# Half a line of 64 bytes ahead of the weight units and of one half of h

## The chip, the cores and the metric

The kernel runs on one core of one Trainium2 chip. The metric is the device time of one execution in microseconds (us), as the median of several runs. On this core TensorE (PE) does the matmuls, with its weight loads shown apart (PEld); VectorE (DVE), ScalarE (ACT) and GpSimd (POOL) do elementwise work; SyncE (SP) issues most of the DMAs.

## The reference

One layer of an encoder on 256 tokens of width 2048, in float32, with post-norm and a residual factor ALPHA = 2**0.25:

```
x <- LN1(ALPHA*x + 0.5 * (silu(x @ w_gate1) * (x @ w_up1)) @ w_down1)      # 2048 -> 5632 -> 2048
p  = x @ w_in                                                              # 2048 -> 6144
y  = [hyena(p[:, :3072]) ; differential attention, 8 heads (p[:, 3072:])]
x <- LN2(ALPHA*x + y @ w_out)
x <- LN3(ALPHA*x + 0.5 * (silu(x @ w_gate2) * (x @ w_up2)) @ w_down2)
```

The two feed-forward blocks (5632 = 44 blocks of 128 wide) hold most of the arithmetic.

## The kernel before

**Float32 products out of rounded halves.** Every operand of a large matmul is held as two tiles of the type float32r: a high half `hi` (ScalarE's cast, L176, L102) and a low half `lo` = value minus `hi` (L177 on VectorE, or L99 on VectorE or GpSimd). A product is three matmuls, high by high, high by low, low by high (`mm3`, L93 to L96).

**Units.** All weights stream through SBUF in units of 512 KB (4,096 bytes in each of the 128 partitions), in an order written out by hand in the list `units`. `fetch` (L158 to L160) puts the DMA of a unit on SP's queue, into one of four `raw` buffers; `prepare` (L172 to L177) splits it into one of four `whi` and one of four `wlo` buffers. `nextunit` asks for transfers five units ahead and for splits two units ahead. The splits of four of the last eight units go into room of `xx` instead.

**Two ways round.** In the gate and up projections of both feed-forward blocks (groups `ps`) and in the Hyena part of w_in (groups `ph`), `ws_block` makes the weight unit the stationary operand and the turned x the moving one. `xx` holds, for each of 16 blocks of 128 features, the high half (256 tokens) and the low half (256 tokens) side by side, so that two matmuls do the three products: 512 columns with the unit's high half (L395) and 256 columns with its low half (L396). In the down projections (`pd`), the attention part of w_in (`pa`) and w_out (`pwo`) it is the other way round: the stationary operand is a block of tokens of `hh` and `hl` (the two halves of the feed-forward's h), of `xx`, or of the mixer's outputs, and the unit moves, 512 or 256 columns at a time, through the three matmuls L94 (high, high), L95 (high, unit's low) and L96 (low, unit's high).

**What else runs.** Beside the stream of matmuls, the generators in `side` are stepped once for each unit: filters and Hyena's transforms, softmax, layer norms, gates. Temporaries of 2,048 bytes share eight buffers with the tag `t512`.

**Places.** SBUF is given out pool by pool, in a row: `const`, then `wp` (the units), then `sm` (first the `t512` buffers, then `space`, then the smaller temporaries), then the pool of the stage (`fp` of a feed-forward block with `hh` and `hl`, or the pools of the mixer). A tile called `space` is written and read by nobody; it only moves what follows:

```
    line(const, 384 - 32 - 256)
    ...
    line(sm, 384)
```

In the program of before, all tiles that this change touches begin at a multiple of 128 bytes in the partition: `xx` at 35,328, the `raw`, `whi` and `wlo` buffers from 68,096 on in steps of 4,096, `t512` from 117,248 on, `hh` at 138,752 and `hl` at 183,808. The slices of them that a matmul reads lie whole multiples of 512 bytes behind these starts.

Of the kernel before, what the change touches and what calls it, by code (L numbers as in the profile page):

```python
# [11 lines left out]
F32 = mybir.dt.float32  # L12
# [5 lines left out]
P = 128  # L18
# [56 lines left out]
def kernel(ctx: ExitStack, tc: tile.TileContext, a: dict, out: bass.AP):  # L75
    nc = tc.nc

    const = ctx.enter_context(tc.tile_pool(name="const", bufs=1))
    wp = ctx.enter_context(tc.tile_pool(name="wp", bufs=4))
    sm = ctx.enter_context(tc.tile_pool(name="sm", bufs=2))  # L80
# [3 lines left out]
    def bank(name):  # L84
        return psp.tile([P, 512], F32, tag="ps", name=name)

    def line(pool, n):

        pool.tile([P, n // 4], F32, name="space", tag="space", bufs=1)

    mm = nc.tensor.matmul

# [8 lines left out]
    def split(o_hi, o_lo, x, eng=None):  # L101
        nc.scalar.copy(out=o_hi, in_=x)  # L102
        sub(eng or nc.vector, o_lo, x, o_hi)
# [85 lines left out]
    def beside(gen):  # L189
        side.append([0, gen])  # L190
# [11 lines left out]
    def once(f, *args):  # L202
        def g():
            f(*args)
            return
            yield
        beside(g())

    def nextunit():
        i = st["use"]  # L210
        st["use"] += 1
        fetch(i + 1 + AHEAD)
        prepare(i + 1 + READY)
        tick()
        return parts.pop(i)

    def finish_side():
        while side:
            tick()


    mhalf = const.tile([P, 2], F32, name="mhalf")
    stats = const.tile([P, 2, 5, 6], F32, name="stats")
    line(const, 384 - 32 - 256)
    ident = const.tile([P, P], F32, name="ident")
    ones = const.tile([P, P], F32, name="ones")
# [2 lines left out]

    res = const.tile([P, 2, D], F32, name="res")  # L230
    xx = const.tile([P, KD, 2, L], F32R, name="xx")
    xv = a["x"][0].rearrange("(p j) d -> p j d", j=2)
    xt0 = []
    for kp in range(KD // 2):
# [6 lines left out]
        if kp % 2 == 0:  # L241
            fetch(kp // 2 + 1)

    line(sm, 384)
    make_identity(nc, ident)
    nc.gpsimd.memset(ones, 1.0)
    nc.gpsimd.memset(mhalf, -0.5)
# [112 lines left out]
    def last_rows(tag, pd, scale, between=None):  # L360

        ln = []
        add_rows(pd[0], 0, 3, scale)
        ln.append(ln_stats(tag, 0))
        for half in range(2):
            add_rows(pd[1][half], 1, 3, scale, half)
            if between is not None and half == 0:
                between()
        ln.append(ln_stats(tag, 1))
        if tag == "2":  # L370
            warm(WARM)
        return ln
# [14 lines left out]
    def ws_block(ps, h, lo, kq, between=None):  # L387

        for k in range(4):
            kk = kq * 4 + k  # L390
            if k == 2 and between is not None:
                between()
            for t in range(2):
                ts_ = slice(t * P, (t + 1) * P)
                mm(out=ps[t], lhsT=h[:, k, ts_], rhs=xx[:, kk].rearrange("p a l -> p (a l)"), start=kk == 0, stop=False)  # L395
                mm(out=ps[t][:, :L], lhsT=lo[:, k, ts_], rhs=xx[:, kk, 0, :], start=False, stop=kk == KD - 1)  # L396

    def ws_sum(o, ps):
        nc.scalar.copy(out=o, in_=ps[:, L:])
        nc.vector.tensor_tensor(out=o, in0=ps[:, :L], in1=o, op=ALU.add)  # L400
# [18 lines left out]
    def last_banks(name):  # L419
        return [bank(f"{name}_0"), [bank(f"{name}_1{h}") for h in range(2)]]  # L420

    def as_chunk(pd, lhs, n_k, lead=1):

        n = n_k // 2
        for ku in range(n - lead):
            as_block(pd, lhs, [(ku * 2, nextunit())], n_k)
        use = [(ku * 2, nextunit()) for ku in range(n - lead, n)]
        as_block(pd, lhs, use, n_k, True)


    def ffn(tag, first, down_side=None, gate_side=None, filler=None, lead=2, between=None):
        with tc.tile_pool(name=f"ffn{tag}", bufs=1, reuse_waits="tile") as fp:
            hh = fp.tile([P, KF, L], F32R, name=f"hh{tag}")
            hl = fp.tile([P, KF, L], F32R, name=f"hl{tag}")

            def gate(f, pg, pu):
                sg = sm.tile([P, L], F32, tag="sg", name=f"sg{tag}_{f}")
                ws_sum(sg, pg)
                nc.scalar.activation(out=sg, in_=sg, func=AF.Silu)
                hf = sm.tile([P, L], F32, tag="hf", name=f"hf{tag}_{f}")  # L440
                ws_sum(hf, pu)
                nc.gpsimd.tensor_tensor(out=hf, in0=hf, in1=sg, op=ALU.mult)  # L442
                split(hh[:, f, :], hl[:, f, :], hf, nc.gpsimd)

            first(0)
            for fb in range(FF // 256):
                if fb == 12 and gate_side is not None:
                    beside(gate_side)
                ps = [[bank(f"ps{tag}_{fb}_{m}_{t}") for t in range(2)] for m in range(2)]
                for kq in range(4):  # L450
                    for m in range(2):
                        more = fb == 0 and kq < 3 and m == 0
                        ws_block(ps[m], *nextunit(), kq, (lambda: first(kq + 1)) if more else None)
                for t in range(2):
                    once(gate, fb * 2 + t, ps[0][t], ps[1][t])
            if down_side is not None:
                beside(down_side)

            def lhs(k, j):
                js = slice(j * P, (j + 1) * P)  # L460
                return hh[:, k, js], hl[:, k, js]

            for c in range(4):
                pd = [bank(f"pd{tag}_{c}_{j}") for j in range(2)] if c < 3 else last_banks(f"pd{tag}_{c}")
                as_chunk(pd, lhs, KF, lead if c == 3 else 1)
                if c < 3:
                    for j in range(2):
                        once(add_rows, pd[j], j, c, 0.5)
            finish_side()
            if filler is not None:  # L470
                filler()
            return last_rows(tag, pd, 0.5, between)
# [173 lines left out]
    def rows_of_x():  # L646
# [4 lines left out]
        yield from scale_residual("0", None, None)  # L651

    ln = ffn("1", first0, filter_gen(), filter_net(), fill)
    xn1 = dr.tile([P, 2, D], F32, name="xn1")

# [419 lines left out]
    def last_side():  # L1075
        yield from last_vectors()
        yield 1
        ln_rows()

    ln = ffn("3", first2, last_side(), lead=LEAD, between=early_g)  # L1080
    ov = out[0].rearrange("(p j) d -> p j d", j=2)

# [57 lines left out]
```

## Time and profile before

| | |
|---|---|
| median of 3 runs | 1944.33 us (1944.19 to 1946.62) |
| the profiled execution: its own time | 1943.8 us |
| its span, first to last instruction | 1942.0 us |
| granted TensorE clock | 0.998 |
| PE busy | 1922.5 us, 99% of the span, 10,582 matmul records |
| DVE, ACT, POOL busy | 63%, 48%, 16% |
| DMA | 376.50 MB, 194 GB/s on average |

The profile's rows name an instruction by its line (L395), engine, operation and tiles (out<-in). A group's row gives the count, the busy time in us, the mean of one instruction in ns, and the idle time of the engine ahead of them with what ended it. Matmuls are pipelined: the duration of one is longer than the distance from its start to the next one's start, and it is the distance that counts for the time.

### The profile page before, as it was taken

To read this page: it belongs to the slowest core of one execution; us is meant where nothing else is said; L and a number is where in the kernel's file an instruction comes from. 1 tells how busy PE (TensorE), PEld (TensorE's weight loads), DVE (VectorE), ACT (ScalarE), POOL (GpSimd) and SP (SyncE) were. 2 spreads that over 40 slices of the span, in tenths; PEclk is the share of its full clock that TensorE was granted. 3 is DMA by queue.
4 is the path that set the end of the run, shared out by engine and by line. 5 is a ranking of instruction groups with operands and counts; after the bars stand their busy time and mean duration, and the time that the engine had idled before them with its cause. 6 is when DMAs were issued, how large, how long until landed. Compare 5 with 4: busy or idle time off the path is not lost. (4 is left out here: it accounts for less than half of the span.)

```text
span 1942.0 us, 27741 instructions
## 1 busy us (share of the span) xinstructions
PE 1922.5 (99%) x10582; PEld 1659.8 (85%) x10582; DVE 1214.3 (63%) x1552; ACT 925.7 (48%) x1336; POOL 302.9 (16%) x335
## 2 busy tenths in 40 slices
PE   9999999999999999999999999999999999999998
PEld 8888888888888888888888888888888888888887
DVE  5555556555566656899978766755555555545545
ACT  5454444455444434554555544545444455433332
POOL 4212111112100001112222011311211112200000
PEclk9999999999999999999999999999999999999999
DMA  8665656565666665755575444856665655566653
GB/s 289 203 194 185 194 187 199 187 193 185 205 207 227 212 190 198 234 181 166 175 218 165 160 157 158 279 188 192 188 193 187 193 187 187 189 199 195 194 188 129
DMA packets 295278, 376.50 MB, mean 194 GB/s; under 512 B 13583, under 2 KB 223144, under 8 KB 295144
## 3 DMA queue, kind: packets, MB, share of 16 engines
q1 hardware_dynamic: 289720, 361.37, 58.5%
q0 software_dynamic: 4992, 12.82, 2.1%
q8 instruction: 83, 1.36, 0.3%
q10 hardware_dynamic: 432, 0.52, 0.1%
q14 instruction: 51, 0.42, 0.1%
HBM read 366.28 MB, written 8.39 MB: 193 GB/s over the span
## 5 line engine op out<-in xcount | busy, mean ns | idle before, releaser
L395 PE MATMUL ps<-xx,hi1g 128*128 128x512 f32 x1408 | 489.8, 394 | 0.8 <-ACT hi1g L176 0.8
L395 PE MATMUL ps<-xx,hi2g 128*128 128x512 f32 x1408 | 488.6, 394 | 1.1 <-DVE xx L99 1.1
L396 PE MATMUL ps<-xx,lo1g 128*128 128x256 f32 x1408 | 391.5, 279 | 1.1 <-DVE lo1g L177 1.1
L396 PE MATMUL ps<-xx,lo2g 128*128 128x256 f32 x1408 | 390.0, 277 | 0.0
L177 DVE TENSOR_TENSOR lo2g<-raw2g,hi2g 128x1024 fp32r<-128x1024 f32 x176 | 235.0, 1337 | 179.6 <-ACT hi2g L176 179.6
L177 DVE TENSOR_TENSOR lo1g<-raw1g,hi1g 128x1024 fp32r<-128x1024 f32 (+1 forms) x180 | 232.7, 1295 | 178.4 <-ACT hi1g L176 178.2
L395 PEld LDWEIGHTS ps<-xx,hi2g 128*128 128x128 f32 x1408 | 264.0, 188 | 62.5 <-ACT xt L305 1.3
L395 PEld LDWEIGHTS ps<-xx,hi1g 128*128 128x128 f32 x1408 | 263.8, 188 | 62.1 <-ACT hi1g L176 1.5
L176 ACT CAST hi2g<-raw2g 128x1024 fp32r<-128x1024 f32 x176 | 185.2, 1053 | 186.6 <-PE ps L395 174.9
L176 ACT CAST hi1g<-raw1g 128x1024 fp32r<-128x1024 f32 (+1 forms) x180 | 185.8, 1034 | 180.9 <-PE ps L395 170.4
L396 PEld LDWEIGHTS ps<-xx,lo1g 128*128 128x128 f32 x1408 | 265.2, 188 | 2.2 <-DVE lo1g L177 1.9
L396 PEld LDWEIGHTS ps<-xx,lo2g 128*128 128x128 f32 x1408 | 264.2, 188 | 0.1
L442 POOL TENSOR_TENSOR hf<-hf,sg 128x256 f32<-128x256 f32 x88 | 65.3, 761 | 741.9 <-DVE hf L400 741.8
L177 DVE TENSOR_TENSOR lo2d<-raw2d,hi2d 128x1024 fp32r<-128x1024 f32 x84 | 103.3, 1229 | 111.2 <-ACT hi2d L176 111.0
L176 ACT CAST hi1d<-raw1d 128x1024 fp32r<-128x1024 f32 x88 | 92.6, 1053 | 127.5 <-PE pd L96 117.0
L177 DVE TENSOR_TENSOR lo1d<-raw1d,hi1d 128x1024 fp32r<-128x1024 f32 x88 | 107.3, 1222 | 69.6 <-ACT hi1d L176 69.6
L176 ACT CAST hi2d<-raw2d 128x1024 fp32r<-128x1024 f32 x84 | 88.6, 1054 | 130.1 <-PE pd L96 123.2
L95 PE MATMUL pd<-lo1d,hh 128*128 128x512 f32 (+1 forms) x396 | 145.2, 367 | 0.0
L94 PE MATMUL pd<-hi1d,hh 128*128 128x512 f32 (+1 forms) x396 | 145.1, 366 | 0.0
L96 PE MATMUL pd<-hi1d,hl 128*128 128x512 f32 (+1 forms) x396 | 144.8, 366 | 0.0
L395 PE MATMUL ph<-xx,hihy 128*128 128x512 f32 x384 | 136.9, 400 | 2.1 <-DVE xx L99 1.1
L95 PE MATMUL pd<-lo2d,hh 128*128 128x512 f32 (+1 forms) x372 | 137.3, 369 | 0.0
(387 smaller groups left out, 3151.9 us busy)
## 6 DMA issues: line engine op xcount, KB each, us to landing
raw1d<-in_ffn_w_down_dram SPq DMA_DIRECT2D x88, 512.0 KB, 3.9
raw2g<-in_ffn_w_gate_dram SPq DMA_DIRECT2D x88, 512.0 KB, 3.5
raw2g<-in_ffn_w_up_dram SPq DMA_DIRECT2D x88, 512.0 KB, 3.4
raw2d<-in_ffn_w_down_dram SPq DMA_DIRECT2D x88, 512.0 KB, 4.1
raw1g<-in_ffn_w_gate_dram SPq DMA_DIRECT2D x87, 512.0 KB, 4.2
raw1g<-in_ffn_w_up_dram SPq DMA_DIRECT2D x87, 512.0 KB, 3.9
rawhy<-in_w_in_dram SPq DMA_DIRECT2D x48, 512.0 KB, 4.0
rawat<-in_w_in_dram SPq DMA_DIRECT2D x48, 512.0 KB, 4.2
```

The source lines that it names most:

```text
L94: mm(out=o, lhsT=lh, rhs=rh, start=start, stop=False)
L95: mm(out=o, lhsT=lh, rhs=rl, start=False, stop=False)
L96: mm(out=o, lhsT=ll, rhs=rh, start=False, stop=stop)
L176: i1 = nc.scalar.copy(out=hi[:, s_], in_=raw[:, s_])
L177: i2 = nc.vector.tensor_tensor(out=lo[:, s_], in0=raw[:, s_], in1=hi[:, s_].bitcast(F32), op=ALU.subtract)
L395: mm(out=ps[t], lhsT=h[:, k, ts_], rhs=xx[:, kk].rearrange("p a l -> p (a l)"), start=kk == 0, stop=False)
L396: mm(out=ps[t][:, :L], lhsT=lo[:, k, ts_], rhs=xx[:, kk, 0, :], start=False, stop=kk == KD - 1)
L442: nc.gpsimd.tensor_tensor(out=hf, in0=hf, in1=sg, op=ALU.mult)
```

## The change

Three tiles of padding are changed; no instruction is added, removed or moved. A tile of 64 bytes, tag `half`, comes behind `xx` in the pool `const`, so that all of `wp` and the `t512` buffers of `sm` begin 64 bytes later: in the middle of a line of 128 bytes. The padding in `sm` becomes 64 bytes shorter, so that everything behind it stays where it was. A second tile of 64 bytes comes between `hh` and `hl`.

```
-    def line(pool, n):
-        pool.tile([P, n // 4], F32, name="space", tag="space", bufs=1)
+    def line(pool, n, tag="space"):
+        pool.tile([P, n // 4], F32, name=tag, tag=tag, bufs=1)
...
     xx = const.tile([P, KD, 2, L], F32R, name="xx")
+
+    line(const, 64, "half")
...
-    line(sm, 384)
+    line(sm, 320)
...
             hh = fp.tile([P, KF, L], F32R, name=f"hh{tag}")
+            line(fp, 64, "half")
             hl = fp.tile([P, KF, L], F32R, name=f"hl{tag}")
```

So `raw`, `whi`, `wlo`, `t512` and `hl` begin half a line in; `xx`, `hh`, the small temporaries and all tiles of the mixer stay at whole lines.

## The prediction, made before the changed kernel ran

> **What bounds the kernel now.** I read the page's busy times first, then PE's waits, then the stages, and last PE's timeline, since a change of places alone can only act through the time that one instruction or one transfer takes.
>
> ```profile
> span 1942.0 us, 27741 instructions
> ...
> PE 1922.5 (99%) x10582; PEld 1659.8 (85%) x10582; DVE 1214.3 (63%) x1552; ACT 925.7 (48%) x1336; POOL 302.9 (16%) x335
> ...
> PEclk9999999999999999999999999999999999999999
> ```
>
> PE is busy in all but 19.5 of 1942.0 us, at full clock. The waits of PE, longest first, show how little of it stands for others:
>
> ```profile
> PE pn L1101 <- DVE nm L1099: 2.8, 1, 2.8
> PE py L94 <- ACT rha L102: 2.6, 1, 2.6
> ...
> PE ps L396 <- DVE lo1g L177: 1.1, 2, 0.5
> ```
>
> After "<-" stands what ended the wait, then its total, its count and its longest. No wait for a unit's split is longer than 0.5 us. The busy times by stretch (from:to, length, PE, PEld, DVE, ACT, POOL, each with its count, then PE's clock, the DMA share and GB/s) show a gate stage and a down stage:
>
> ```profile
> 1220.00:1680.00 460.00, 460.00 (x2657) 402.06 (x2656) 262.75 (x265) 226.52 (x335) 85.90 (x95) 1.00 0.63 198
> 1700.00:1860.00 160.00, 160.00 (x707) 132.51 (x707) 76.43 (x68) 62.25 (x59) 0.00 (x0) 1.00 0.61 194
> ```
>
> PE has no idle time in either. So the time is the number of matmuls times the distance from one start to the next, which PE's timeline gives. First down, 512 columns each:
>
> ```profile
> 1699.82 0.39 PE L95 MATMUL pd<-lo2d,hh 128*128 128x512 f32 x1
> 1700.04 0.39 PE L96 MATMUL pd<-hi2d,hl 128*128 128x512 f32 x1
> 1700.27 0.39 PE L94 MATMUL pd<-hi2d,hh 128*128 128x512 f32 x1
> ...
> 1701.18 0.39 PE L95 MATMUL pd<-lo2d,hh 128*128 128x512 f32 x1
> ```
>
> From L95 to the second L95 after it are 6 matmuls in 1.36 us: 226.7 ns each. Then matmuls of 256 columns near the end, 27 from the first row to the last:
>
> ```profile
> 1919.95 0.28 PE L94 MATMUL pd<-xx,hh 128*128 128x256 f32 x1
> ...
> 1923.18 0.28 PE L94 MATMUL pd<-hi2d,hh 128*128 128x256 f32 x1
> ```
>
> 3.23 us by 27 is 119.6 ns. The difference, 107 ns for 256 columns, is 0.418 ns a column, so a matmul costs its columns times 0.418 ns and a fixed 12.5 to 13 ns. The gates agree, with 8 pairs of 512 and 256 columns between these two rows:
>
> ```profile
> 1499.72 0.40 PE L395 MATMUL ps<-xx,hi2g 128*128 128x512 f32 x1
> 1499.95 0.28 PE L396 MATMUL ps<-xx,lo2g 128*128 128x256 f32 x1
> ...
> 1502.49 0.40 PE L395 MATMUL ps<-xx,hi2g 128*128 128x512 f32 x1
> ```
>
> 2.77 us by 8 is 346.2 ns; 226.7 and 119.6 are 346.3. So the same two numbers hold in both stages, though POOL works through one and stands still in the other, and though VectorE is at 57% in the one and 48% in the other: what other engines read and write in SBUF doesn't show in PE's pace.
>
> **The change part by part.** No instruction is added, removed or moved, and no queue gets another order. Each part asks only whether an instruction of a known count becomes longer or shorter.
>
> (a) Units as moving operand, half a line in. The counts are in the groups by shape, one row of the three lines L94 to L96 each:
>
> ```profile
> L94 PE MATMUL pd<-hi1d,hh 128*128 128x512 f32 x308 | 120.3, 391 | 0.0
> ...
> L94 PE MATMUL pd<-hi2d,hh 128*128 128x512 f32 x300 | 116.9, 390 | 0.0
> ...
> L94 PE MATMUL pd<-hi1d,hh 128*128 128x256 f32 x88 | 24.8, 282 | 0.0
> L94 PE MATMUL pwo<-hiwo,yhh 128*128 128x512 f32 x56 | 22.6, 404 | 0.0
> ...
> L94 PE MATMUL pd<-hi2d,hh 128*128 128x256 f32 x72 | 20.3, 282 | 0.0
> ...
> L94 PE MATMUL pa1k<-hiat,xx 128*128 128x512 f32 x32 | 13.1, 410 | 0.0
> ```
>
> Down has 3 x (308 + 300) = 1,824 of 512 and 3 x 160 = 480 of 256 columns; w_out has two groups of 56 (`yhh` and the like for the attention half) on three lines, 336; the attention part of w_in has 6 sections of 3 x 32, 576. That makes some 3,200 matmuls. No row of this trace reads a moving operand from the middle of a line, so the price is bounded. Dearer: a row of 512 columns covers 16 lines from a line's start and 17 from its middle; if PE took whole lines, it would pay the half line that it reads in vain, 16 columns or 6.7 ns, up to a whole line, 13.4 ns: 21 to 43 us. Cheaper: the fixed 13 ns could go at most. I take 0, because the columns already pass at a steady 0.418 ns whatever else happens, so nothing shows that reading holds them back.
>
> (b) Units as stationary operand, half a line in.
>
> ```profile
> L395 PE MATMUL ps<-xx,hi1g 128*128 128x512 f32 x1408 | 489.8, 394 | 0.8 <-ACT hi1g L176 0.8
> ...
> L396 PE MATMUL ps<-xx,lo1g 128*128 128x256 f32 x1408 | 391.5, 279 | 1.1 <-DVE lo1g L177 1.1
> L396 PE MATMUL ps<-xx,lo2g 128*128 128x256 f32 x1408 | 390.0, 277 | 0.0
> L396 PEld LDWEIGHTS ps<-xx,lo1g 128*128 128x128 f32 x1408 | 265.2, 188 | 2.2 <-DVE lo1g L177 1.9
> ...
> L395 PE MATMUL ph<-xx,hihy 128*128 128x512 f32 x384 | 136.9, 400 | 2.1 <-DVE xx L99 1.1 <-POOL xx L99 1.0
> ```
>
> L395 and L396 have 1,408 each in both blocks and 384 each in Hyena's part: 6,400 weight loads from units, of 188 ns. A load reads 512 bytes, 4 lines or, from the middle, 5. It lies beside the matmul ahead of it: two loads of 188 ns in a pair of 346 ns are themselves pipelined, so I can't read the slack from their durations. Dearest: a quarter more, 47 ns, shown in full behind the 3,200 short matmuls only, 150 us. Cheapest: the fixed 13 ns gone, 83 us for 6,400. I take 0, the nearest rows being the pairs themselves: at 119.6 ns the 256-column matmul shows the same fixed part as the long one, so the load isn't what sets the short one's pace now.
>
> (c) `hl` half a line in: it is the stationary operand of L96, a third of the matmuls of down, and counts within (a): 0, between the same ends.
>
> (d) The splits and the gates' tail. ScalarE's casts and VectorE's subtractions read and write units half a line in, GpSimd writes `hl` there.
>
> ```profile
> L177 DVE TENSOR_TENSOR lo2g<-raw2g,hi2g 128x1024 fp32r<-128x1024 f32 x176 | 235.0, 1337 | 179.6 <-ACT hi2g L176 179.6
> ...
> L176 ACT CAST hi2g<-raw2g 128x1024 fp32r<-128x1024 f32 x176 | 185.2, 1053 | 186.6 <-PE ps L395 174.9
> ...
> L712 DVE SCALAR_TENSOR_TENSOR z<-pc,pvt,z 128x128 f32<-128x128 f32 x48 | 18.0, 414 | 4.2 <-ACT z L705 4.2
> ...
> L712 DVE SCALAR_TENSOR_TENSOR z<-pc,pvt,z 128x127 f32<-128x127 f32 x48 | 14.5, 341 | 0.0
> ```
>
> The last two rows are the nearest to a shifted operand: the second form starts one element, 4 bytes, into its operand on one side, and takes no longer than the first (341 against 414 ns). One line more on 32 would be 3%, 40 ns on 1,337; it lies inside the idle time at the end of each row (VectorE 179.6 us ahead of 176 instructions). Where VectorE is nearly full, in the Hyena stage, 48 subtractions at 40 ns would be 2 us; so 0, with 2 us as the upper end, and as much below.
>
> (e) Transfers into `raw` and `t512`, half a line in.
>
> ```profile
> raw2g<-in_ffn_w_gate_dram SPq DMA_DIRECT2D x88, 512.0 KB, 3.5
> ...
> raw1g<-in_ffn_w_gate_dram SPq DMA_DIRECT2D x87, 512.0 KB, 4.2
> ```
>
> ```profile
> SPq L160 <- DVE lo2g L177: 367.7, 154, 11.6
> ```
>
> A unit lands 3.5 to 4.2 us after its issue, and SP's queue itself waits for a free `raw` (second fence, from the waits of SP). A buffer comes free when the subtraction of its unit ends, and its next unit is split four units later: 4 x 8 pairs x 346 ns is 11.1 us, less the cast and the subtraction (1.05 and 1.34 us), 8.7 us. A transfer twice as long would still be in time. Only the first units, at the start, are waited for: 0, up to 1 us. [...]
>
> The sum: 0 in all five parts. The profiled execution took 1943.8 us, 1.8 over its span and 0.5 below the median of 1944.33; I forecast 1944.3 us.
>
> **The rivals.** 0.2%, 3.9 us, is about what a measurement of this kernel can tell from no change.
>
> *Slower, whole lines for the moving operand (part a).* For it: 13 ns is 31 columns, close to the 32 of one line, as if each matmul read one line too many. Against it: the rows give the same 13 ns to operands that begin exactly at a line, and the attention's matmuls, with half the rows of the array and the same 256 columns, are shorter (below). It gives 1944.3 + 21 = 1965 us with the half line, 1987 with a whole one. It decides from 1.2 ns a matmul on.
>
> ```profile
> L96 PE MATMUL psc<-qh,ql 64*128 64x256 f32 x32 | 6.7, 276 | 0.0
> ...
> L96 PE MATMUL po<-wh,vl 128*128 128x256 f32 x16 | 4.5, 282 | 0.0
> ```
>
> 276 against 282 ns for the same lines speaks for a fixed part that lies in the array, not in SBUF. The same rival can act through the weight loads (part b); then 3,200 x 5 ns already gives 1960 us.
>
> *Faster, weight load and moving operand on opposite halves.* If the fixed 13 ns is a load that collides with the moving row while both begin at a line, then the gates (unit half a line in, `xx` not) and two thirds of down are now set apart. For it: the 13 ns are the same at 512 and 256 columns, as one load of the same size in each would give. Against it: that PE's pace doesn't feel the other engines, and that start offsets hardly keep two streams of different speed apart. All of it on 9,600 matmuls is 125 us, 1819 us; a fifth, 2.7 ns, is 26 us, 1918 us. It decides from 0.4 ns on. [...]
>
> *Slower through transfers or splits.* One place: the first unit and the Hyena stage, 1 + 2 us: 1947 us, inside the bound of no change, and so counted there.
>
> **How the numbers follow.** No change, 0.58: both rows of pace hold with any neighbours. Slower by whole lines or dearer loads, 0.22, half of it beyond the half line's 21 us. Faster by opposite halves, 0.20, half of it beyond 26 us. Leaving out the outer half on either side (0.10 and 0.11) gives 1918 to 1966 us; the likeliest case's own range is 1941 to 1948.
>
> **What the changed profile would show.** If I am right, the starts in down stay 226.7 ns apart and a pair of the gates 346 ns. If the slower rival holds, down's starts lie 233 or 240 ns apart and the gates' pair stays. If loads are dearer, the pair grows and down's 512-column matmuls stay. If the faster rival holds, the pair falls below 346 ns first, and down's L94 and L95 before L96. What would make the prediction wrong is any change of these distances by more than 0.4 ns, since nothing else in the kernel stands between PE and the end.

## The result, and the profile after

The changed kernel takes 1967.9 us (median of 4 runs, 1966.79 to 1969.21), the kernel before beside it on the same chip 1944.82 us: the medians are 23 us apart, and the ratio on record is 1.0111 [1.0097 to 1.0125]. The forecast was 1944.3 us, and the range ended at 1966.

The head of the page after:

```profile
span 1966.8 us, 27741 instructions
...
PE 1945.1 (99%) x10582; PEld 1667.8 (85%) x10582; DVE 1213.5 (62%) x1552; ACT 925.3 (47%) x1336; POOL 304.0 (15%) x335
...
PEclk9999999999999999999999999999999999999999
```

The counts are the same, the granted clock is 0.998 in both, and most of what the span grew by is busy time of PE (1945.1 - 1922.5 = 22.6 us of 24.8). The other engines' times stand. So the same 10,582 matmuls became slower. The long waits of PE are the same ones at the same lengths, save one: at the start, the wait for `xx` came twice and took 2.8 us, where before it took 1.1 (second fence, from before):

```profile
PE ps L397 <- DVE xx L99: 2.8, 2, 1.7
PE pn L1104 <- DVE nm L1102: 2.8, 1, 2.8
PE py L94 <- ACT rha L102: 2.6, 1, 2.6
```

```profile
PE ps L395 <- DVE xx L99: 1.1, 1, 1.1
```

The timeline of PE in the second gate stage, after (start, duration, line, operation, tiles; L397 and L398 are the lines that were L395 and L396):

```profile
1522.70 0.40 PE L397 MATMUL ps<-xx,hi2g 128*128 128x512 f32 x1
1522.93 0.28 PE L398 MATMUL ps<-xx,lo2g 128*128 128x256 f32 x1
...
1525.52 0.40 PE L397 MATMUL ps<-xx,hi2g 128*128 128x512 f32 x1
```

Eight pairs lie between the first row and the last: 2.82 us, 352.5 ns a pair, where before had 346.2. Then down, 512 columns, after:

```profile
1724.72 0.39 PE L95 MATMUL pd<-lo2d,hh 128*128 128x512 f32 x1
...
1726.10 0.39 PE L95 MATMUL pd<-lo2d,hh 128*128 128x512 f32 x1
```

Six matmuls in 1.38 us, 230 ns each, against 226.7. And the 256 columns near the end, 27 matmuls:

```profile
1944.21 0.28 PE L94 MATMUL pd<-xx,hh 128*128 128x256 f32 x1
...
1947.40 0.28 PE L94 MATMUL pd<-hi2d,hh 128*128 128x256 f32 x1
```

3.19 us by 27 is 118.1 ns, *less* than the 119.6 before. So a place costs something in one kind of matmul and saves something in another.

Summed over the whole trace, the distances from start to start give the account: the 3,200 pairs of gates and Hyena's part took 1119.2 us before and 1139.8 after (+20.6), down's 512-column matmuls 414.8 and 418.0 (+3.2), all else together about +1. That is the 24.8 us of the span. Of the 20.6, the 2,816 pairs of the gates have 20.1 (at 6.67 ns each 18.8, the rest mostly the longer wait for `xx`). Hyena's 384 pairs have only 0.5, because most of them ran as slowly before; their rows stand near the end.

To read the pace finely, I take the distance from start to start, averaged over a stretch, less 0.4167 ns for each column: the run table below has 226.7 ns at 512 columns and 120.0 at 256 with both operands at 0, and 106.7 by 256 is 0.4167. What is left is called the fixed part below. In the long even stretches before, it is 13.3 ns for each matmul: 26.7 for the gates' pair, 40.0 for down's three. After, it is 33.3 for the pair and 46.7 for the three of 512 columns, but 33.3 for the three of 256 columns.

### The profile page after: what moved, and what is told of

The parts are those of the page before. It is cut to its first block, busy times and chain, and to the rows that moved or that the text cites. A ratio compares the mean times of both kernels' runs of the same rounds, so it can differ in the third digit from the quotient of the medians.

```text
span 1966.8 us, 27741 instructions
## 1 busy us (share of the span) xinstructions
PE 1945.1 (99%) x10582; PEld 1667.8 (85%) x10582; DVE 1213.5 (62%) x1552; ACT 925.3 (47%) x1336; POOL 304.0 (15%) x335
## 5 line engine op out<-in xcount | busy, mean ns | idle before, releaser
L397 PE MATMUL ps<-xx,hi1g 128*128 128x512 f32 x1408 | 498.2, 398 | 2.3 <-DVE xx L99 1.7
L397 PE MATMUL ps<-xx,hi2g 128*128 128x512 f32 x1408 | 497.9, 398 | 1.1 <-DVE xx L99 1.1
L398 PE MATMUL ps<-xx,lo1g 128*128 128x256 f32 x1408 | 395.3, 281 | 1.7 <-DVE lo1g L177 1.7
L398 PE MATMUL ps<-xx,lo2g 128*128 128x256 f32 x1408 | 395.6, 281 | 0.0
L177 DVE TENSOR_TENSOR lo2g<-raw2g,hi2g 128x1024 fp32r<-128x1024 f32 x176 | 233.9, 1330 | 186.7 <-ACT hi2g L176 186.7
L397 PEld LDWEIGHTS ps<-xx,hi1g 128*128 128x128 f32 x1408 | 264.4, 188 | 68.7 <-ACT hi1g L176 3.2
L397 PEld LDWEIGHTS ps<-xx,hi2g 128*128 128x128 f32 x1408 | 264.6, 188 | 66.4 <-ACT xt L307 1.3
L398 PEld LDWEIGHTS ps<-xx,lo1g 128*128 128x128 f32 x1408 | 264.2, 188 | 3.1 <-DVE lo1g L177 2.9
L398 PEld LDWEIGHTS ps<-xx,lo2g 128*128 128x128 f32 x1408 | 264.3, 188 | 0.1
L397 PE MATMUL ph<-xx,hihy 128*128 128x512 f32 x384 | 137.4, 399 | 2.2 <-DVE xx L99 1.1
L94 PE MATMUL pd<-hi2d,hh 128*128 128x512 f32 (+1 forms) x372 | 138.2, 371 | 0.0
```

The costliest lines, as they stand in the source:

```text
L94: mm(out=o, lhsT=lh, rhs=rh, start=start, stop=False)
L177: i2 = nc.vector.tensor_tensor(out=lo[:, s_], in0=raw[:, s_], in1=hi[:, s_].bitcast(F32), op=ALU.subtract)
```

## The experiments

Two theories at the start. **R**: what counts is the place of the operand being loaded *relative to* that of the operand being streamed (the load of the next weights lies beside the current stream: in the timeline of before, L396's load and L395's matmul ahead of it both start at 1499.72 us). **A**: each operand pays for its own place, whatever the other's. Every timed kernel ran beside the kernel before on the same chip; before's median was 1944.8 to 1946.3 us in these groups. Edits are shown against the kernel before, where it isn't said otherwise. The tables are kernels with matmuls alone on fixed data; they leave out the whole layer, so only their distances are read, and each ran once.

**table: one load and one stream, at each place.**

```
for so in places: for mo in places:
    48 x matmul(out=ps[:, :cols], lhsT=st[:, so + 128 q : ...], rhs=mv[:, mo + cols q : ...])
```

> Only matmuls, none of the layer: stretches of 48 (pairs: 64) float32r matmuls back to back on fixed data, each with its own places of the loaded (stationary) and the moving operand: 0, 32, 64, 96 or 128 bytes into a line of 128, 512 or 256 columns, then the gates' pair and down's three. What counts is the distance from start to start less 0.4167 ns a column; it is 13.3 ns where both begin at a line, as in the kernel before. Theory R (the relative place of the two operands counts): 13.3 ns again with both at 64; with loaded 0 and moving 64 it is 20.0 ns at 512 and 6.7 ns at 256 columns, with loaded 64 and moving 0 it is 26.7 and 6.7 ns, as the changed kernel's stretches hint; 128 equals 0. Theory A (each operand pays for itself): 16.7 ns for every loaded operand at 64 whatever the moving one's place, and a fixed surcharge for a moving one at 64 that is the same at 512 and 256 columns and never below 13.3.

Its timeline on PE; a tile's name is columns (w 512, n 256), place of the loaded operand, place of the streamed one (a 0, b 32, c 64, e 128 bytes), and a row is 48 matmuls:

```profile
17.95 11.04 PE L80 MATMUL waa<-mv,st 128*128 128x512 f32 x48
28.83 11.37 PE L80 MATMUL wab<-mv,st 128*128 128x512 f32 x48
40.03 11.16 PE L80 MATMUL wac<-mv,st 128*128 128x512 f32 x48
...
128.92 11.07 PE L80 MATMUL wcc<-mv,st 128*128 128x512 f32 x48
139.82 11.37 PE L80 MATMUL wcd<-mv,st 128*128 128x512 f32 x48
...
206.74 11.30 PE L80 MATMUL wae<-mv,st 128*128 128x512 f32 x48
217.88 11.05 PE L80 MATMUL wee<-mv,st 128*128 128x512 f32 x48
228.76 5.92 PE L80 MATMUL naa<-mv,st 128*128 128x256 f32 x48
234.52 5.82 PE L80 MATMUL nab<-mv,st 128*128 128x256 f32 x48
...
274.32 5.61 PE L80 MATMUL nca<-mv,st 128*128 128x256 f32 x48
279.77 5.84 PE L80 MATMUL ncb<-mv,st 128*128 128x256 f32 x48
```

From one start to the next: both at 0, 10.88 us or 226.7 ns a matmul; both at 64, 10.90 us; both at 128, 10.88 us. Stream 32 bytes further than the load, 11.20 us or 233.3 ns. With 64 bytes between them 229 (stream further) or 233 ns. Even 128 bytes between them give 11.14 us, 232 ns. At 256 columns it goes the other way: equal places 5.76 us or 120.0 ns, load 64 bytes further 5.45 us or 113.5 ns. So theory A falls: equal places cost the same wherever they lie, are the fastest at 512 columns and the slowest at 256. Two places at the same difference agree within 1 ns, with one exception: at 256 columns a load 64 bytes further took 113.5 ns at (64, 0), loaded place first, but 117.7 at (96, 32). That 128 bytes are not the same as 0 was not expected, and of R's four figures for places 64 bytes apart only one came (6.7 ns expected, 6.9 measured, at (64, 0) and 256 columns; at 512 columns 26.7 was expected there and 20.0 came).

The same table also ran the gates' pair, with all operands at 0 (rows below, 31 pairs apart):

```profile
336.78 0.39 PE L80 MATMUL pairaaa<-mv,st 128*128 128x512 f32 x1
...
347.73 0.40 PE L80 MATMUL pairaaa<-mv,st 128*128 128x512 f32 x1
```

10.95 us by 31 is 353.2 ns, a fixed part of 33.3: the changed kernel's pace at before's places. With both units 64 bytes further it was 33.3 too. So this table doesn't tell before from the change in the gates, and single streams don't add up to a pair: at (64, 0) the two alone have 20.0 and 6.9 ns, together 26.9, while at (0, 0) they have 26.7. What the places do to a pair is left to the runs that follow.

**units_half: the units alone half a line in.**

```
+    line(const, 64, "half")       # behind xx
-    line(sm, 384)
+    line(sm, 320)
```

> The change without the second padding tile: units and t512 half a line in, hl at a whole line. Theory R: gates as in the changed kernel (+21 us on before); in down all three matmuls have the loaded operand at 0 and the moving one at 64, 20.0 ns over the columns at 512, so some 8 us more than the changed kernel there and 2 us less in its 256-column part: 1974 us. Theory A: hl costs 3.3 ns less on a third of down's matmuls: 1965 us.

1969.93 us, ratio 1.0123 [1.0108 to 1.0138]: as slow as the change as a whole. The gates' pair has the same 33.3 ns as in the change. Down's three run at two paces, one in each feed-forward block:

```profile
599.75 0.40 PE L94 MATMUL pd<-hi1d,hh 128*128 128x512 f32 x1
...
606.75 0.40 PE L94 MATMUL pd<-hi1d,hh 128*128 128x512 f32 x1
...
1726.22 0.39 PE L94 MATMUL pd<-hi2d,hh 128*128 128x512 f32 x1
...
1728.97 0.39 PE L94 MATMUL pd<-hi2d,hh 128*128 128x512 f32 x1
```

Ten threes in 7.00 us are 700 ns each, a fixed part of 60.0 as theory R expected; four in 2.75 us are 687.5, and over the whole second down the fixed part is 46.7. The order and the places of the operands are the same in both. The two downs together are 3.5 us longer than before.

**hl_half: `hl` alone.**

```
             hh = fp.tile([P, KF, L], F32R, name=f"hh{tag}")
+            line(fp, 64, "half")
             hl = fp.tile([P, KF, L], F32R, name=f"hl{tag}")
```

> The other part alone: only hl half a line in, units at whole lines. Gates as before by both theories (346.7 ns a pair). Theory R: one of three loads in down stands against a moving operand at the other half, 13.3 ns more per three at 512 columns (608 of them, +8 us) and 6.7 ns less per three at 256 (160, -1 us): 1951 us. Theory A: 3.3 ns per three, 1947 us.

1952.66 us, ratio 1.0033 [1.0021 to 1.0045]. The gates keep their pace, the two downs are 2.9 and 3.5 us longer, near theory R's 1951 us and not A's 1947. Timeline of PE in down:

```profile
1704.69 0.39 PE L94 MATMUL pd<-hi2d,hh 128*128 128x512 f32 x1
...
1706.08 0.39 PE L94 MATMUL pd<-hi2d,hh 128*128 128x512 f32 x1
```

Six in 1.39 us, 231.7 ns. The parts don't add up. On down's 512-column matmuls, units alone cost 6.1 us (420.9 for 414.8), `hl` alone 7.0 (421.8), both together 3.2 (418.0). With both moved, `hl` and the unit are at equal places again; that this is why `hl`'s cost goes away is argued, not shown, and half of what units alone cost is the slow pace of the first block.

**all_half: every tile behind the first padding half a line in, `xx` and `hh` too.**

```
-    line(const, 384 - 32 - 256)
+    line(const, 384 - 32 - 256 + 64)
```

> The same 64 bytes ahead of everything: ident, res, xx, the units, t512, the small temporaries, hh, hl and all tiles of the mixer begin half a line in, so that no operand stands otherwise against another than in the kernel before. Theory R: 1944 us, gates' pair 346.7 ns, down 226.7 ns. Theory A: at least the 23 us of the changed kernel, since units are loaded from mid-line in the gates and move from mid-line in down, and xx and hh now lie there too: 1968 us or more.

1946.28 us, ratio 1.0000 [0.9990 to 1.0009]. Timeline of PE in the second gate stage, 7 pairs:

```profile
1499.64 0.40 PE L395 MATMUL ps<-xx,hi2g 128*128 128x512 f32 x1
...
1502.07 0.39 PE L395 MATMUL ps<-xx,hi2g 128*128 128x512 f32 x1
```

2.43 us by 7 is 347 ns, before's pace, with not one of these operands at the start of a line. So a start in the middle of a line of 128 bytes isn't what costs the time (ratio 1.0000); the place of one operand against the other's is (units alone moved: 1.0123).

**table_gates and table_down: the real sequences, at coarse places.**

```
for hi in places: for lo in places:  gates' pairs: 512 columns with whi at hi, 256 with wlo at lo; xx at 0
for hl in (0, 64, 128): for hi in places: for lo in places:  down's three; hh at 0
```

> Only the gates' matmuls, in their order and with places that agree with the kernel's in all but the start of the two halves of a unit: the high half 0 to 512 bytes further than x, the low half 0 to 512 bytes further, every pair of eleven distances, 40 pairs of matmuls each. Counted is the pair's time over its columns (320 ns). Both at 0: 26.7 ns as in the kernel before; both at 64: 33.3 ns as in the changed kernel. If only the place in a line of 128 bytes counts (theory R1), 128, 256, 384 and 512 give 26.7 again. If the distance itself counts (theory R2), 128 gives about 31 ns as the first table's 19.1 and 12.0 do, and some distances give less than 26.7.

> Only down's three matmuls of 512 columns (high by high, high by the unit's low, low by the unit's high), in their order, with hl 0, 64 or 128 bytes off hh's place and the unit's two halves at seven distances each. Counted is the time of three over their columns (640 ns). All at 0: 40 ns as before. Both halves of the unit and hl at 64: 46.7 ns as in the changed kernel; the same with hl at 0 is what the run with units alone shows. R1: 128 and 256 give 40. R2: they don't, and some give less than 40.

Fixed part of the gates' pair in ns, rows the place of the high half, columns that of the low half (bytes against `xx`):

```
        0      64     128    192    256
  0    26.7   26.7   26.7   31.1   33.3
 64    20.0   33.3   30.0   33.3   20.0
128    32.0   33.3   31.1   26.7   32.0
192    30.0   26.7   26.7   33.3   30.0
256    26.7   26.7   26.7   31.1   33.3
```

The table has before's 26.7 at (0, 0) and the change's 33.3 at (64, 64). The rows of 256 and of 512 repeat that of 0, the row of 384 that of 128. Down's three have their least, 40.0, with all places equal (`hl`, high half, low half at 0, 0, 0; 0, 256, 256 has nearly as little), 46.7 at (64, 64, 64) and about 57 at (0, 128, 128). Some places don't fit a rule of places alone: (0, 0) and (0, 256) differ though 256 bytes apart, (192, 0) has 30.0 and (448, 0), not shown above, 20.0, and (64, 0) has 20.0, well below before.

**units_128 and units_256: is the period 128 or 256 bytes?** Units at the start of a line in both.

```
+    const.tile([P, 32], F32, name="half")      # units_256: [P, 64]
-    line(sm, 384)
+    line(sm, 256)                              # units_256: line(sm, 128)
```

> As the run with units alone, but a whole line: units and t512 begin 128 bytes later than before, still at the start of a line, everything else in place. R1 (only the place in a line counts): 1945 us, pair 346.7 ns. R2 (the distance counts): by the first table's 19.1 ns at 512 and 12.0 ns at 256 columns for 128 bytes apart, 4.4 ns a pair on 3,200 pairs is 14 us, 5.8 ns on 2,700 matmuls of 512 columns with a moving unit is 16 us, 1 us less on those of 256: 1974 us.

> Units and t512 256 bytes later than before, everything else in place. The two tables of the stages repeat after 256 bytes of distance: both halves of the unit 256 off x give 33.3 ns a pair in the gates' table although the high half alone at 256 gives 26.7, so two readings: with a period of 256 bytes throughout, 1946 us as before (pair 346.7 ns); with the table's own corner (256, 256), 33.3 ns a pair, +6.7 ns on 3,200 pairs, 1967 us.

128 bytes: 1968.53 us, ratio 1.0117 [1.0100 to 1.0134], as slow as the half line. 256 bytes: 1945.79 us, ratio 0.9999 [0.9990 to 1.0009]. The second gate stage's windows (from:to, length, PE busy with its count, then PEld, DVE, ACT, POOL, PE's clock, DMA share, GB/s) count how many matmuls pass in 180 us. Before:

```profile
1500.00:1680.00 180.00, 180.00 (x1041) 157.34 (x1040) 98.73 (x97) 87.51 (x129) 30.59 (x32) 1.00 0.60 190
```

The changed kernel:

```profile
1500.00:1680.00 180.00, 180.00 (x1021) 156.36 (x1020) 96.29 (x96) 86.54 (x128) 30.64 (x32) 1.00 0.59 186
```

units_128:

```profile
1500.00:1680.00 180.00, 180.00 (x1027) 157.74 (x1026) 97.42 (x97) 86.45 (x128) 30.53 (x32) 1.00 0.62 188
```

units_256:

```profile
1500.00:1680.00 180.00, 180.00 (x1040) 157.42 (x1039) 98.61 (x98) 87.56 (x129) 30.59 (x32) 1.00 0.62 190
```

1,041, 1,021, 1,027 and 1,040 matmuls: 128 bytes are not the same as 0, and 256 are, so in this kernel the period is 256 bytes. In units_128 the gates' pair has a fixed part of 31.1 ns and down's three of 57 in their long stretches, as in the tables for these places. The tiles that the change touches began at multiples of 256 bytes before.

**hi_64_gates: the table's best place, in the kernel.** The four `whi` become one tile, in which units of 256 columns a row begin 64 bytes further.

```
-                hi = wp.tile([P, k, c], F32R, tag="whi", name=f"hi{name}")
+                o = st["whi"] % 4 * 1024 + (16 if c == 256 else 0)
+                st["whi"] += 1
+                hi = whi[:, o:o + 1024].rearrange("p (k c) -> p k c", k=k)
```

> The four buffers of the units' high half become slices of one tile, 64 bytes later for units of 256-column blocks (gates, up, Hyena's part of w_in) and at the old distance for the others; raw and the low half keep their distance from x. In the gates' table this place (high half 64 off, low half and x together) has 20.0 ns over the columns of a pair against 26.7. Theory R2: 340.0 ns a pair, 6.7 ns on 3,200 pairs, 21 us faster: 1925 us; down unchanged. If a steady state of the table isn't that of the kernel: 1946 us.

1949.72 us, ratio 1.0017 [0.9987 to 1.0047], with single runs from 1935.5 to 1959.6: neither of the two expected values, and no one value at all. (In this kernel 16 columns of a unit's high half are overwritten early where the unit's kind changes, so some of its values are wrong; the number and shape of its matmuls stay. The two later kernels with these places skip a slot there.) Its timeline, early and late:

```profile
149.72 0.39 PE L398 MATMUL ps<-xx,whi 128*128 128x512 f32 x1
...
152.44 0.39 PE L398 MATMUL ps<-xx,whi 128*128 128x512 f32 x1
...
1500.05 0.39 PE L398 MATMUL ps<-xx,whi 128*128 128x512 f32 x1
...
1502.85 0.39 PE L398 MATMUL ps<-xx,whi 128*128 128x512 f32 x1
```

Eight pairs each: 2.72 us or 340.0 ns (fixed part 20.0) at 150 us, 2.80 us or 350.0 ns (30.0) at 1500 us, with the same instructions at the same places. The pace went from 20.0 to 30.0 behind the filters' small matmuls at 291 us and stayed there to the end of the stage. A third theory, **S**, follows: at one place there are several steady paces, and how the stream began decides which of them holds.

**table_gates16 and table_down16: 256 combinations in steps of 16 bytes.**

```
-OFF = {c: 8 * i for i, c in enumerate("abcdefghijklmnopq")}    # in elements of 4 bytes
+OFF = {c: 4 * i for i, c in enumerate("abcdefghijklmnop")}
```

> The gates' table in steps of 16 bytes from 0 to 240, 24 pairs each. R2 with places that count in pieces of 64 bytes: the values of the coarse table, in blocks of 4 by 4. R2 with finer pieces: other values between, with 20.0 ns or less in places not yet seen.

> Down's table with hl in hh's place, in steps of 16 bytes from 0 to 240, 12 times three matmuls each. Both at 0: 40 ns over the columns of three. If 13.3 ns a matmul is the least that 512 columns allow, no place falls below 40; else some do.

The gates' pair takes 20.0 to 35.0 ns, median 29.4; only 5 of 256 are below 26. (64, 0) has 33.3 here, where the coarse table has 20.0: the same place again at another pace. Down's three take 40.0 to 86.8, median 54.8, and only 4 of 256 have the 40.0 of equal places; none is below. For down, before's places were as good as any.

**table_entry: each place entered in 12 ways**, by other matmuls just ahead.

```
+    KICKS = [(), (128,), (192,), (256,), (320,), (384,), (448,), (512,), (128, 128), ...]
+        for i in range(len(kick)):
+            mm(out=pk[:, :kick[i]], lhsT=h[:, 0, :P], rhs=xx[:, :kick[i]], start=True, stop=True)
```

> Is the pace set by the places alone, or also by the way in which the stream of matmuls comes in? The gates' pairs at four places (high and low half of the unit 0, 0; 64, 64; 64, 0; 128, 128 bytes off x) and down's three at four (hl, high, low: 0,0,0; 64,64,64; 0,64,64; 0,128,128), each twelve times, with nothing or one to six matmuls of 128 to 512 columns put ahead. Theory P (places alone): the same value twelve times at each place: gates 26.7, 33.3, 20.0, 31.1 ns a pair, down 40, 46.7, 46.7 ns a three. Theory S (several steady states at each place, entered by chance): two or more values at a place, 20.0 and 30.0 at (64, 0) as in two runs so far, 26.7 and about 33 at (0, 0), each held to the stretch's end.

Two of the 12 streams at (64, 0), with 384 columns ahead and with 448 columns ahead, 16 pairs from the first row to the last of each:

```profile
359.46 0.39 PE L94 MATMUL gca<-xx,whi 128*128 128x512 f32 x1
...
365.06 0.39 PE L94 MATMUL gca<-xx,whi 128*128 128x512 f32 x1
...
370.79 0.39 PE L94 MATMUL gca<-xx,whi 128*128 128x512 f32 x1
...
376.23 0.39 PE L94 MATMUL gca<-xx,whi 128*128 128x512 f32 x1
```

5.60 us or 350.0 ns a pair, and 5.44 us or 340.0. In all, in ns of the fixed part:

```
pair  (0, 0)        26.7 (7 of 12), 33.3 (5)
pair  (64, 64)      33.3 (12)                         the change's gates
pair  (64, 0)       20.0 (2), 30.0 (8), 33.3 (2)
pair  (128, 128)    31.1 to 31.2 (12)
three (0, 0, 0)     40.0 (12)
three (64, 64, 64)  46.7 (12)                         the change's down
three (0, 64, 64)   46.7 (10), 60.0 (2)               units_half's down
three (0, 128, 128) 56.4 to 60.5 (12)
```

S holds: four of the eight places have one pace in all twelve streams, three have two or three, and the last varies by 4 ns. The 46.7 and 60.0 at (0, 64, 64) are the two paces of units_half's two downs. It also sharpens what the change did: at (0, 0) the gates have two paces, and before ran them mostly in the quicker; at (64, 64) only the slow one came. The output's buffer can't be what sets the pace: each block of gates takes four of the eight `ps` buffers, the next block the next four, and the pace held over many blocks (in hi_64_gates 30.0 ns from 316 us to the stage's end).

**hi_64_kick3, hi_64_kick8, kick8_alone: setting the pace on purpose.** The first matmul of some blocks of a gate stage is done twice; the second one, with `start=True` too, writes the same values again. kick3 does so in blocks 1, 2 and 16, kick8 in 1, 2, 4, 8, 12, 16, 18 and 20; the first two have the places of hi_64_gates, the last those of before.

```
+                if twice and k == t == 0:
+                    mm(out=ps[t], lhsT=h[:, k, ts_], rhs=xx[:, kk].rearrange("p a l -> p (a l)"), start=True, stop=True)
```

> The places of the run with the high half 64 bytes off in the gates, and in each feed-forward block the first matmul of 512 columns of three blocks of gates (1, 2 and 16 of 22) done twice, its first result overwritten: in the entry table a matmul of 512 columns put ahead took the stream at (64, 0) from 30.0 to 20.0 ns a pair. Theory S: the stretches of gates hold 20.0 ns from the second block of each stage on, save between the filters' matmuls (block 13) and block 16: some 2,600 pairs at 6.7 ns, -17 us, six matmuls more +1.4 us: 1929 us, and runs that agree. Theory P (20.0 was chance, nothing can be set): runs between 1935 and 1960 us as without the second matmuls.

> The same with the first matmul done twice in eight blocks of gates of each feed-forward block (1, 2, 4, 8, 12, 16, 18, 20): if a disturbance throws the stream out of the 20.0 ns state on the way, this brings it back. Theory S: 16 matmuls more, +3.6 us, at most 1 us gained over three of them: 1931 us. Should one of the added matmuls itself throw the stream out, the blocks behind it show 30.0 ns until the next.

> The eight blocks' second matmuls alone, all places as before. In the entry table 512 columns put ahead led to 26.7 ns a pair at (0, 0), the state in which the kernel before already runs its long stretches. Theory S: +3.6 us, less what the blocks with 34 ns behind the filters' matmuls get back (a few us at most): 1946 to 1949 us. If the second matmuls by themselves make gates faster: below 1940.

hi_64_kick3: 1943.52 us, ratio 0.9985 [0.9976 to 0.9993], where 1929 was expected. Its runs agree as expected (1940.4 to 1944.8), and its second gate stage held 20.0 ns and took 482.3 us; but its first ran at 30 to 33 ns nearly throughout, at 499 us for before's 495. (The expectation named 512 columns ahead as what quickened the stream at (64, 0); it was 448, and the stream with 512 ahead came behind it, already quick.) hi_64_kick8: **1937.75 us, ratio 0.9959 [0.9946 to 0.9973], faster than both kernels**, 8 us of some 15 expected. Its second gate stage:

```profile
1499.81 0.39 PE L403 MATMUL ps<-xx,whi 128*128 128x512 f32 x1
...
1502.53 0.39 PE L403 MATMUL ps<-xx,whi 128*128 128x512 f32 x1
```

Eight pairs in 2.72 us, 340.0 ns, throughout the stage, which takes 483.6 us against before's 490.8, with eight matmuls more. In the first gate stage the pace came and went (30.0 to 100 us, 33.3 to 192, 20.0 to 291, 30.0 from 321 to 371, then 20.0), so that nothing was won there. From 40 us on, every lasting change of pace in the gate stages of these three traces lies at a repeated matmul (here those at 101, 192 and 371 us) or at the filters' matmuls, but not every repeated matmul changes the pace: it can change it, it doesn't choose it.

kick8_alone was a miss that tells the most. Expected was no cost beyond 8 matmuls in each stage; measured were 1955.76 us, ratio 1.0054 [1.0040 to 1.0067]:

```profile
1509.84 0.40 PE L397 MATMUL ps<-xx,hi2g 128*128 128x512 f32 x1
...
1512.66 0.40 PE L397 MATMUL ps<-xx,hi2g 128*128 128x512 f32 x1
```

Eight pairs in 2.82 us, 352.5 ns, exactly the pace of the changed kernel, with every tile where it was before. The slow pace began at the repeated matmul of block 1 (1230 us) and ended at that of block 18 (1616 us). The second gate stage took 500.0 us for 490.8. Its eight added matmuls are 1.8 us of that, so the pace alone, at unchanged places, moves the time of one stage by some 7 us.

## Why the prediction was wrong, point by point

**What bounds the kernel: right.** PE without gaps (99% busy), the time as a sum of distances from start to start, and but for 1.7 us on `xx` at the start no wait that grew by more than 0.6 us.

**(b), units as stationary operand, taken at 0: this is the step that failed.** It measured +6.67 ns on each of the gates' 2,816 pairs, 19 of the 24.8 us (20.6 with Hyena's pairs and the wait for `xx`), inside the bounds (83 cheaper to 150 dearer) and far from the value taken. The reason given, that the 256-column matmul shows the same fixed part as the 512-column one, "so the load isn't what sets the short one's pace now", doesn't follow. The fixed part itself changes with the places of load and stream: the table has it at 6.9 ns (256 columns, 113.5 ns, load 64 bytes further) as well as at 20.0 (512 columns). In place of an unchanged pair, the gates' pair has two paces at before's places, 26.7 and 33.3 ns over its columns, and at the change's places all twelve streams and both gate stages ran at 33.3.

**(a) and (c), units as moving operand and `hl`, taken at 0:** down's 512-column matmuls measured +3.2 us together, against bounds from 21 us dearer for a half line read in vain. The reason, that a column takes 0.418 ns "whatever else happens", was again too wide: the run table has 0.417 ns from 256 to 512 columns at equal places (120.0 and 226.7 ns), but 0.468 with the load 64 bytes further (113.5 and 233.3 ns). The two were not independent, as the sum took them: 6.1 us alone, 7.0 alone, 3.2 together.

**(d) and (e): right.** Groups of the page after:

```profile
L177 DVE TENSOR_TENSOR lo2g<-raw2g,hi2g 128x1024 fp32r<-128x1024 f32 x176 | 233.9, 1330 | 186.7 <-ACT hi2g L176 186.7
...
raw2g<-in_ffn_w_gate_dram SPq DMA_DIRECT2D x88, 512.0 KB, 3.6
```

The subtraction took 1,330 ns (1,337 before), a unit landed in 3.6 us (3.5 for this tile before).

**The sentence on neighbours.** From equal paces beside busy and idle engines I took it that nothing in SBUF is felt by PE. The rows bore on *other* engines only. PE's own two operands, the load and the stream, were the pair in question, and none of the rows that I quoted had them at different places. Nor did the 276 against 282 ns of `psc` and `po` place the fixed part in the array: these are durations, and not distances from start to start (down's 512 columns: 390 ns against 226.7).

Load and stream are not independent of each other: in the run table the same matmul of 512 columns with its load takes 226.7 ns with both at 0 and 233.3 with the load 64 bytes further. Why, no run says.

**The rivals.** "Whole lines" had 1965 us, near the 1967.9 that came, but for a wrong reason in the wrong place: it put 233 or 240 ns on down and left the gates' pair as it was, so the nearness of its number is luck. units_128 (whole lines, slow: 1.0117) and all_half (half lines, not slow: 1.0000) refute it. Its second form, through the weight loads (3,200 x 5 ns, 1960 us), had the right place and nearly the size; but all_half refutes lines as the reason there too. "Opposite halves" named the right two partners, the load against the stream, with a wrong sign at 512 columns (229 and 233 ns with 64 bytes between them, 226.7 at equal places) and a wrong period; at 256 columns its sign was right (113.5 against 120.0 ns at (64, 0)). Of the signs to look for in the changed profile, "if loads are dearer, the pair grows and down's 512-column matmuls stay" came nearest: the pair grew by 1.9% (6.67 of 346.7 ns), down's by 0.8% (3.2 of 414.8 us).

**What I could have seen.** The timeline of before has a slower stretch in the first gate stage:

```profile
300.10 0.40 PE L395 MATMUL ps<-xx,hi1g 128*128 128x512 f32 x1
...
302.91 0.40 PE L395 MATMUL ps<-xx,hi1g 128*128 128x512 f32 x1
```

Eight pairs in 2.81 us, 351.3 ns against the 346.2 that I quoted from 1500 us: about the change's pace, already there behind the filters' small matmuls at 293 us. Most of Hyena's pairs ran so as well, at the same places as the gates':

```profile
845.63 0.40 PE L395 MATMUL ph<-xx,hihy 128*128 128x512 f32 x1
...
848.46 0.40 PE L395 MATMUL ph<-xx,hihy 128*128 128x512 f32 x1
```

Eight pairs in 2.83 us, 353.8 ns; from 846 to 863 us the fixed part is 33.3 ns, exactly the change's. So the slow pace was in the kernel before, and the change could hardly slow this part further. The pace was thus no constant, and the chance of 0.58 for "no change", which rested on "both rows of pace hold with any neighbours", was too high.

**What stays open:** where the period of 256 bytes comes from, what picks the pace when a stream begins, and why a pair at (64, 64) is slower than its two matmuls measured alone. That loads and streams are the partners is shown by their places (226.7 to 233.3 ns in the run table); a matmul without a load of its own was not run.

## What to carry to other kernels

Where PE has no gaps, judge a layout by the distance from start to start, read in several stretches of each stage: if the same matmuls run at two paces, the pace is something to win or lose. Keep the place of the loaded operand and that of the streamed one equal modulo 256 bytes, where nothing measured here beat down's pace at 512 columns (40.0 ns a three, the least in table_down16) and few places beat the gates' (5 of 256 below 26 ns in table_gates16; at 256 columns alone equal places were the slowest, 120.0 ns), or measure a table of the real sequence before moving either; padding that only moves addresses was worth 1% here (ratio 1.0111). A pace that depends on how the stream began can be changed by one extra matmul, in either direction (hi_64_kick8: 33.3 to 20.0 ns a pair at 192 us; kick8_alone: 352.5 ns a pair from 1230 to 1616 us, where before had 346.2), so compare such kernels by the whole trace and not by one stretch.

## What the runs showed of the hardware that I had not expected

- The fixed part of a float32r matmul with a load of its own is no constant: in the run table, alone, it is 13.1 to 14.0 ns at equal places for 512 and for 256 columns, 15.6 to 20.8 at unequal ones for 512, 6.9 to 12.9 for 256.
- What counted in this kernel is the difference of the two places (all of them moved by 64 bytes: ratio 1.0000; units alone: 1.0123), and it counted modulo 256 bytes (units moved by 128: 1.0117; by 256: 0.9999).
- One sequence at one place had up to three steady paces (20.0, 30.0, 33.3 ns a pair at (64, 0) in table_entry), which held for hundreds of us, until other matmuls broke the stream (hi_64_gates: 20.0 to 286 us, the filters' matmuls at 291, 30.0 from 316 to the stage's end).
- Costs of places didn't add: 6.1 (units_half) and 7.0 us (hl_half) apart, 3.2 us together, on down's 512-column matmuls.
